# The seven-product stage of a decoder block: neighbouring pairs interleaved, weights requested further ahead, two tiles for the last sums

## The chip, the cores and the metric

The kernel runs on one core of a Trainium2 chip, as one launch. The time is device microseconds for the whole program. Engines are called as in the profile: PE (TensorE matmuls), DVE (VectorE), ACT (ScalarE), POOL (GpSimd) and SP (SyncE), which here only issues DMAs, from one queue and in order.

## The reference

One decoder block on x of 2048 tokens x 1024 channels, in float32. Two mixers (attention and a gated MLP) are merged and projected, then comes an MLP of width 4096, each with RMSNorm before and after. The stage of the change is the last part, above all the product with w_mlp_in:

```python
y = jnp.einsum('bsd,de->bse', merged, w_out[layer])
x = x + _rmsnorm(y, norm_post_mix[layer])

h = _rmsnorm(x, norm_pre_mlp[layer])
a = jax.nn.relu(jnp.einsum('bsd,df->bsf', h, w_mlp_in[layer]))
y = jnp.einsum('bsf,fd->bsd', a * a, w_mlp_out[layer])
x = x + _rmsnorm(y, norm_post_mlp[layer])
```

## The kernel before

**Precision.** Each float32 operand is split in two parts: a rounded copy (ACT, L71) and the rest (DVE, L76). Every product is three matmuls of such parts, so 128 x 512 outputs over four blocks of 128 channels take twelve.

**The last chunk.** Tokens come in four chunks of 512, in the order 2, 3, 0, 1; a chunk has four blocks of 128 (`out_block`, L764). A block loads x (tile xr), projects with w_out, normalizes, stores x1d (L791), then transposes y (L810) and ACT copies it (L811). In chunks 3 and 1 (`second`) it also loads the same columns of the chunk before from h2_d (L802), POOL makes sums of both (L815 to L818), and five 4-block groups (T1 to T4, B22) are stored to t_d (L820). For chunk 1 all four blocks use the first 20 slices of one tile, `tail`, so a block's loads wait for the store of the block before.

**The first MLP layer.** It is a Strassen-like scheme: the 1024 channels and each pair q of 128-wide weight columns (16 pairs) are halved, and seven products (`TERMS`, L840) take the place of eight. Each token half (half 1, then half 0) needs 16 x 7 = 112 products, 224 in all. For pair q, product 1 (A11 x B11) and 2 (A12 x B21) use bank a; 6, 7 and 4 (S2 x T2, S3 x T3, A22 x T4) bank b; 5 and 3 (S1 x T1, S4 x B22) bank c. A11 and A12 come straight from the raw weights w1r (`first_a`); S1 to S4 and A22 from four POOL sums (`sum_a`, L884 to L887). After 1 ACT copies the bank (xs, L915); after 6 and 7 DVE adds xs (u, L922); outputs are an add on DVE (c, L926), Relu on ACT (L927, or L918 after product 2), a square on POOL (L907) and a store sd (L908). These tiles are called c and form a ring of six.

**What sets the order.** PE runs in the order in which the program calls `product`. For each half this is a lead of five pairs (`ahead`: products 1 and 2 of all five, then `chain`: 6 to 3), a middle, pair by pair 1, 6, 2, 7, 5, 4, 3, and a trail of three pairs like the lead. Weights are made ready six products ahead (`need`), and raw weights are loaded there, into two w1r buffers; pairs of lead and trail load their first half alone (512 KB) and later all of it. The other engines' order, SP's queue too, is laid out by a scheduler from the dependences. Below, "6(0)" is product 6 of pair 0; in tile names the last digits are half and pair (S2_10 is half 1, pair 0; S2_115 half 1, pair 15).

## Time and profile before

| | |
|---|---|
| median of 3 runs | 2910.29 us (2909.26 to 2912.29) |
| the profiled execution | 2906.08 us |
| its span | 2904.3 us (1.78 us lie around it) |
| PE busy | 2802.4 us (96%) |
| DVE, ACT, POOL busy | 1463.8, 858.2, 765.1 us (50%, 30%, 26%) |
| mean granted clock of PE | 0.983 |
| first MLP layer: last matmul of the projection ends, first of the second layer begins | about 1498.6, 2195.14 us |

Times in rows are microseconds from the span's start. A wait is put down to what released it last. "x12" counts instructions that follow each other, and the duration is theirs together. L is a line of the kernel before.

### The profile page before, as it was taken

Reading aid. Unit: us, or ns where it says so; the run is one execution under the profiler, and the core shown is the slowest. Engines: PE = TensorE matmul, PEld = TensorE weight load, DVE = VectorE, ACT = ScalarE, POOL = GpSimd, SP = SyncE. Lnnn points to the kernel's source line nnn. Section 1 sums busy time; section 2 is a strip of 40 time slices with the busy share of each in tenths; the row PEclk is TensorE's granted clock in tenths of the full one; section 3 lists DMA queues with packets and bytes.
Section 4 is the critical chain, followed back from the end, with each engine's and each line's share of the span. In section 5 each row is a group of like instructions: output and inputs, shape, how many; then the busy total and the mean of one; then the engine's idle time right before and its main releaser. Section 6 shows DMA issues by size and latency. Waiting matters only on the chain.

```text
span 2904.3 us, 36721 instructions
## 1 busy us (share of the span) xinstructions
PE 2802.4 (96%) x13748; PEld 2359.1 (81%) x13748; DVE 1463.8 (50%) x2557; ACT 858.2 (30%) x1799; POOL 765.1 (26%) x591
## 2 busy tenths in 40 slices
PE   8999999999999999998987999899999999999998
PEld 8889889888888879787866787777878888888887
DVE  5664562444443354655556553565547444664445
ACT  4213111244443322443434333433332111211111
POOL 0340340200000032113125654265442010320012
PEclk9999999999999999999998999999999999999999
DMA  7544455566666363647456333633345232452232
GB/s 254 176 145 159 152 152 158 156 214 191 198 201 193 134 225 113 217 149 205 135 182 213 113 113 131 196 109 109 116 142 181 80 116 88 138 174 94 88 94 95
DMA packets 246546, 442.89 MB, mean 152 GB/s; under 512 B 17888, under 2 KB 106208, under 8 KB 246368
## 3 DMA queue, kind: packets, MB, share of 16 engines
q1 hardware_dynamic: 246368, 440.55, 47.2%
q8 instruction: 108, 1.77, 0.3%
q14 instruction: 70, 0.57, 0.1%
HBM read 299.77 MB, written 140.71 MB: 152 GB/s over the span
## 4 chain that ended last, share of the span: by engine, by line
PE 77%; DMA 7%; issue 4%; POOL 4%; DVE 4%; ACT 2%; SPq 0%; POOLq 0%; DVEq 0%; ACTq 0%
PE y L87 8%; PE y L86 8%; PE y L88 8%; PE ab L903 6%; PE ac L903 4%; PE aa L903 4%; PE g L86 4%; PE g L88 4%; PE g L87 4%; PE x L87 3%; PE x L86 3%; PE x L88 3%; DMA w1r<-in_w_mlp_in_dram 2%; PE pv L597 2%; DMA g<-gated 1%
## 5 line engine op out<-in xcount | busy, mean ns | idle before, releaser
L87 PE MATMUL y<-w,s 128*128 128x512 f32 x1024 | 400.1, 391 | 0.0
L86 PE MATMUL y<-w,s 128*128 128x512 f32 x1024 | 399.6, 390 | 0.0
L88 PE MATMUL y<-w,s 128*128 128x512 f32 x1024 | 398.8, 389 | 0.0
L71 ACT ACTIVATE s<-s 128x512 fp32r<-128x512 f32 x128 | 80.6, 632 | 495.3 <-DMA s<-sd 467.6
L86 PEld LDWEIGHTS y<-w,s 128*128 128x128 f32 x1024 | 192.3, 188 | 41.1
L88 PEld LDWEIGHTS y<-w,s 128*128 128x128 f32 x1024 | 192.3, 188 | 40.6
L87 PEld LDWEIGHTS y<-w,s 128*128 128x128 f32 x1024 | 192.5, 188 | 39.7
L1109 DVE TENSOR_TENSOR acc<-acc,y 128x512 f32<-128x512 f32 x240 | 159.5, 683 | 129.4 <-PE y L88 129.4
L903 PE MATMUL aa<-B,A 128*128 128x512 f32 x768 | 194.8, 410 | 24.1 <-ACT A L71 12.6
L907 POOL TENSOR_TENSOR c<-c 128x512 f32<-128x512 f32 x126 | 150.7, 1197 | 238.5 <-ACT c L927 176.0
L73 POOL TENSOR_SCALAR w<-w2r 128x1024 fp32r<-128x1024 f32 x64 | 69.6, 1088 | 528.3 <-DVE acc L1109 250.4
L903 PE MATMUL ab<-T,S 128*128 128x512 f32 x768 | 188.6, 398 | 14.6 <-DVE u L922 12.0
L903 PEld LDWEIGHTS aa<-B,A 128*128 128x128 f32 x768 | 151.9, 199 | 60.5 <-ACT A L71 13.6
L903 PEld LDWEIGHTS ab<-T,S 128*128 128x128 f32 x768 | 147.3, 192 | 48.1 <-DVE u L922 13.3
L86 PE MATMUL x<-hT_a,wq 128*128 128x512 f32 x384 | 149.8, 390 | 0.0
L88 PE MATMUL x<-hT_a,wq 128*128 128x512 f32 x384 | 149.6, 390 | 0.0
L87 PE MATMUL x<-hT_a,wq 128*128 128x512 f32 x384 | 149.6, 390 | 0.0
L76 DVE TENSOR_TENSOR A<-w1r,A 128x512 fp32r<-128x512 f32 x92 | 91.7, 1006 | 107.0 <-ACT A L71 106.4
L73 POOL TENSOR_SCALAR w_g<-w_g_r 128x1024 fp32r<-128x1024 f32 x32 | 33.6, 1049 | 411.0 <-PE g L88 329.4
L76 DVE TENSOR_TENSOR w<-w2r,w 128x1024 fp32r<-128x1024 f32 x64 | 82.2, 1285 | 115.6 <-POOL w L73 115.6
L604 DVE TENSOR_REDUCE o<-po 128x256 f32<-128x512 f32 x48 | 33.2, 691 | 184.1 <-PE po L603 184.1
L76 DVE TENSOR_TENSOR s<-s 128x512 fp32r<-128x512 f32 x128 | 90.0, 710 | 70.2 <-ACT s L71 69.9
(276 smaller groups left out, 6531.2 us busy)
## 6 DMA issues: line engine op xcount, KB each, us to landing
w1r<-in_w_mlp_in_dram SPq DMA_DIRECT2D x32, 1024.0 KB, 5.3
w2r<-in_w_mlp_out_dram SPq DMA_DIRECT2D x64, 512.0 KB, 3.6
s<-sd SPq DMA_DIRECT2D x128, 256.0 KB, 4.6
sd<-c SPq DMA_DIRECT2D x126, 256.0 KB, 2.7
qk<-hl SPq DMA_DIRECT2D x24, 1024.0 KB, 5.3
qq<-qk SPq DMA_DIRECT2D x96, 256.0 KB, 5.0
w_g_r<-in_w_in_dram SPq DMA_DIRECT2D x32, 512.0 KB, 5.3
gated<-gt SPq DMA_DIRECT2D x64, 256.0 KB, 3.1
```

The source lines that it names most:

```text
L71: act.activation(hi, src, AF.Copy)
L73: pool.tensor_scalar(hi, src, 1.0, 1.0, op0=OP.mult, op1=OP.mult)
L76: (pool if lo_eng == "pool" else dve).tensor_sub(lo, src, f32(hi))
L86: pe.matmul(ps, lh, rh, start=start, stop=False)
L87: pe.matmul(ps, lh, rl, start=False, stop=False)
L88: pe.matmul(ps, ll, rh, start=False, stop=stop)
L597: pe.matmul(pv[:, o0:o0 + w_], l, r, start=n == 0, stop=n == len(mms) - 1, skip_group_check=True)
L604: dve.tensor_reduce(ot[:, :, j * 64:(j + 1) * 64], po.rearrange("p (b h e) -> p b e h", b=4, h=2), axis=AX.X, op=OP.add)
L903: pe.matmul(p, w[:, l, k, :], h[:, r, k, :], start=i in (1, 6, 5) and not k and not n, stop=k == 3 and n == 2, skip_group_check=True)
L907: pool.tensor_mul(t, t, t)
L1109: dve.tensor_add(an, an, p)
```

## The change

It edits the last chunk's blocks, the loading of weights and the order of the products; no product is added or left out.

- The h2_d loads of a block are issued with its xr load; the t_d store becomes a third part of the block, run by `store()`. Chunk 1 alternates between two 20-slice parts of `tail`, which has 48 slices instead of 44.
- For pairs of lead and trail A11 and A12 are loaded apart, 256 KB each (`lone_a`), into c tiles; the first five of half 1 go through the last eight slices of `tail`, A11 of pair 2 among them.
- w1r has three buffers instead of two, and its loads are asked for 14 products ahead (`raw_need`); splits and sums still six ahead. A pair of lead or trail loads w1r once, whole.
- `places` gives every product a place in a list; both halves' lists are put into one by sorting. The T tiles are loaded in the order T2, T3, T1, T4, B22 (before T2, T1, T3, T4, B22).

```diff
--- before.py
+++ after.py
@@ -767,6 +767,12 @@
         isl = slice(i * P, (i + 1) * P)
         xt = tp.tile([P, D], F32, name=f"xr_{c}{i}", tag="xr", bufs=1)
         sp.dma_start(xt, x[t0:t0 + P, :])
+        second = c % 2
+        if second:
+
+            tt = tt_tile(c, i)
+            for o in range(2):
+                sp.dma_start(tt[:, 3 * o], h2_d[:, o * 4:o * 4 + 4, t0 - 512:t0 - 512 + P])
...
@@ -794,12 +800,6 @@
...
-        second = c % 2
-        if second:
-
-            tt = tt_tile(c, i)
-            for o in range(2):
-                sp.dma_start(tt[:, 3 * o], h2_d[:, o * 4:o * 4 + 4, t0 - 512:t0 - 512 + P])
...
@@ -816,16 +816,23 @@
...
+        yield
+        if second:
             dst = t_d[c // 2].rearrange("p o k t -> p (o k) t")[:, :, i * P:(i + 1) * P]
             sp.dma_start(dst, tt.rearrange("p o k t -> p (o k) t"))
         yield
 
-    last = [None]
+    last, stores = [None], []
 
     def flush():
         if last[0]:
             next(last[0])
+            stores.append(last[0])
             last[0] = None
+
+    def store():
+        while stores:
+            next(stores.pop(0))
 
     chunks = (2, 3, 0, 1)
     e3, er = ExitStack(), ExitStack()
@@ -859,23 +866,31 @@
...
+    def lone_a(half, q, n, raw=None):
+
+        w = r3.tile([P, 2, 4, P], F32R, name=f"A1{n + 1}_{half}{q}", tag="wh", bufs=5)
+        if raw is None:
+            raw = cp3.tile([P, 512], F32, name=f"ar{n}_{half}{q}", tag="c", bufs=6)
+            raw = raw.rearrange("p (k c) -> p k c", k=4)
+        split_in(w, a["w_mlp_in"][2 * q][:, n * 4:n * 4 + 4], raw, "act")
+        a_[half, q, f"A1{n + 1}"] = w
+
+    def first_a(half, q):
 
         for n, name in enumerate(("A11", "A12")):
             w = r3.tile([P, 2, 4, P], F32R, name=f"{name}_{half}{q}", tag="wh", bufs=5)
-            split(w[:, 0], w[:, 1], raw[:, n * 4:n * 4 + 4], "act", "dve")
+            split(w[:, 0], w[:, 1], araw[half, q][:, 0, n * 4:n * 4 + 4], "act", "dve")
             a_[half, q, name] = w
 
-    def load_a(half, q, n=2):
-
-        raw = wp3.tile([P, 2, KT, P], F32, name=f"w1r_{half}{q}", tag="w1r", bufs=2)
-        sp.dma_start(raw[:, :n].rearrange("p f k c -> p f (k c)"),
-                     a["w_mlp_in"][2 * q:2 * q + n].rearrange("f p k c -> p f (k c)"))
+    def load_a(half, q):
+        raw = wp3.tile([P, 2, KT, P], F32, name=f"w1r_{half}{q}", tag="w1r", bufs=3)
+        sp.dma_start(raw.rearrange("p f k c -> p f (k c)"),
+                     a["w_mlp_in"][2 * q:2 * q + 2].rearrange("f p k c -> p f (k c)"))
         araw[half, q] = raw
 
     def sum_a(half, q):
 
-        raw = araw.pop((half, q))
+        raw = araw[half, q]
...
@@ -934,19 +949,33 @@
...
-    def chain(qs, between):
-
-        o = [(qs[0], 6)]
-        for n, q in enumerate(qs):
-            o += [(q, 5), (q, 7)] + ([(qs[n + 1], 6)] if n + 1 < len(qs) else between) + [(q, 4), (q, 3)]
-        return o
-
-    def ahead(qs):
-
-        o = [(q, 1) for q in qs]
-        for n, q in enumerate(qs):
-            o.insert(min(2 * n + 2, len(o)), (q, 2))
-        return o
+    def places(half):
+
+
+
+        o = []
+
+        def ahead(qs, t0):
+            o.extend((t0 + t, q, 1) for t, q in zip((0, 1, 3, 5, 7), qs))
+            t = dict(zip(qs, (2, 4, 6, 8, 9)))
+            o.extend((t0 + t[q], q, 2) for q in qs)
+
+        def chain(qs, t0):
+            for n, q in enumerate(qs):
+                o.extend((t0 + 5 * n + t, q, i) for i, t in ((6, 0), (7, 3), (5, 4), (4, 6), (3, 7)))
+
+        ahead(range(LEAD), 0)
+        t0 = 2 * LEAD - 2.5
+        chain(range(LEAD), t0)
+        t0 += 5 * LEAD
+        for q in range(LEAD, NQ - TRAIL):
+            o.extend((t0 + t, q, i) for i, t in ((1, -0.25), (6, 1.25), (2, 3), (7, 5), (5, 6), (4, 9), (3, 11)))
+            t0 += 7
+        trail = range(NQ - TRAIL, NQ)
+        ahead(trail, t0 + 0.25)
+        t0 += 2 * TRAIL
+        chain(trail, t0)
+        return o, t0 + 5 * TRAIL
 
...
@@ -967,7 +996,7 @@
 
     def tt_tile(c, i):
         if c == 1:
-            return tail[:, :20].rearrange("p (o k) t -> p o k t", o=5)
+            return tail[:, i % 2 * 20:i % 2 * 20 + 20].rearrange("p (o k) t -> p o k t", o=5)
...
@@ -975,75 +1004,76 @@
     mg = merge(2, yt, {}, spatial_out)
     for n, c in enumerate(chunks):
         if n:
-            mg = merge(c, yt, {2: flush})
+            mg = merge(c, yt, {2: flush, 5: store})
         if n < 3:
             yt = load_y(chunks[n + 1])
         for i in range(4):
+            store()
+            if n == 3 and i == 0:
+                tail = yp.tile([P, 48, P], F32, name="tail", tag="yt")
             b = out_block(c, i, mg)
             next(b)
             flush()
             last[0] = b
-            if n == 3 and i == 0:
-                tail = yp.tile([P, 44, P], F32, name="tail", tag="yt")
             if n == 3 and i == 1:
                 e2r.close()
...
-                rw = tail[:, 20:].rearrange("p (n k) c -> p n k c", n=3)
-                for q in range(2):
-                    sp.dma_start(rw[:, q], a["w_mlp_in"][2 * q])
-                    first_a(1, q, rw[:, q])
-                    rls.append(rw[:, 2, q * 4:(q + 1) * 4].rearrange("p k t -> p (k t)"))
+                rls += [gtp.tile([P, 512], F32, name=f"c11_{o}", tag=f"gt{o}", bufs=2) for o in range(2)]
+                for o, (q, n_) in enumerate(((0, 0), (1, 0), (0, 1), (1, 1), (2, 0))):
+                    lone_a(1, q, n_, tail[:, 40 + o % 2 * 4:44 + o % 2 * 4])
 
 
     first_half, second_half = 1, 0
     for q, i in ((0, 1), (1, 1), (0, 2), (1, 2)):
         product(first_half, q, i)
     flush()
+    store()
     e2.close()
     ea = ExitStack()
...
-    order = []
-    for half in (first_half, second_half):
-        lead, trail = list(range(LEAD)), list(range(NQ - TRAIL, NQ))
-        o = ahead(lead) + chain(lead, [(LEAD, 1)])
-        for q in range(LEAD, NQ - TRAIL):
-            o += [(q, i) for i in (1, 6, 2, 7, 5, 4, 3) if (q, i) != (LEAD, 1)]
-        o += ahead(trail) + chain(trail, [])
-        order += [(half, q, i) for q, i in o if half != first_half or q > 1 or i > 2]
+    o, t_end = places(first_half)
+    order = [(t, first_half, q, i) for t, q, i in o if q > 1 or i > 2]
+    order += [(t + t_end, second_half, q, i) for t, q, i in places(second_half)[0]]
+    order = [z[1:] for z in sorted(order)]
 
     ends = {}
     for z in order:
         if z[0] == first_half:
             ends[TERMS[z[2]][1]] = z
-    have = {(first_half, q): {1} for q in range(2)}
+    have = {(first_half, 0, 1), (first_half, 1, 1), (first_half, 0, 2), (first_half, 1, 2), (first_half, 2, 1)}
+
+    def alone(q):
+        return q < LEAD or q >= NQ - TRAIL
 
     def need(half, q, i):
 
-        h = have.setdefault((half, q), set())
-        part = 1 if i < 3 else 2
-        if part in h:
+        if (half, q, i) in have:
             return
-        h.add(part)
-        alone = q < LEAD or q >= NQ - TRAIL
-        if part == 1:
-            load_a(half, q, 1 if alone else 2)
-            first_a(half, q, araw[half, q][:, 0])
-            if alone:
-                araw.pop((half, q))
+        if i < 3 and alone(q):
+            lone_a(half, q, i - 1)
+            have.add((half, q, i))
+        elif i < 3:
+            first_a(half, q)
+            have.update(((half, q, 1), (half, q, 2)))
         else:
-            if (half, q) not in araw:
-                load_a(half, q)
             sum_a(half, q)
-
-    tops = ["T2", "T1", "T3", "T4", "B22"]
+            have.update((half, q, n) for n in range(3, 8))
+
+    def raw_need(half, q, i):
+        if (half, q) not in araw and not (i < 3 and alone(q)):
+            load_a(half, q)
+
+    tops = ["T2", "T3", "T1", "T4", "B22"]
     for n, z in enumerate(order):
         if tops:
             load_t(first_half, tops.pop(0))
+        for z2 in order[n:n + 14]:
+            raw_need(*z2)
         for z2 in order[n:n + 6]:
             need(*z2)
         product(*z)
```

On PE, at the start of the first half, the kernel before ran all products 1 and 2 of the lead and then pair 0's 6 (ab_10 with T2), 5 (ac_10 with T1) and 7 (T3):

```order
L903 MATMUL aa_13_13330<-B11_1_12923,A11_13_13272 128x512 x12
L903 MATMUL aa_12_13286<-B21_1_12930,A12_12_13267 128x512 x12
L903 MATMUL aa_14_13375<-B11_1_12923,A11_14_13280 128x512 x12
L903 MATMUL aa_13_13330<-B21_1_12930,A12_13_13275 128x512 x12
L903 MATMUL aa_14_13375<-B21_1_12930,A12_14_13283 128x512 x12
L903 MATMUL ab_10_13451<-T2_1_13255,S2_10_13310 128x512 x12
L903 MATMUL ac_10_13466<-T1_1_13301,S1_10_13312 128x512 x12
L903 MATMUL ab_10_13451<-T3_1_13345,S3_10_13311 128x512 x12
L903 MATMUL ab_11_13520<-T2_1_13255,S2_11_13399 128x512 x12
L903 MATMUL ab_10_13451<-T4_1_13368,A22_10_13313 128x512 x12
```

And now, from the same product 1(3) on:

```order
L918 MATMUL aa_13_13343<-B11_1_12924,A11_13_13274 128x512 x12
L918 MATMUL aa_12_13314<-B21_1_12931,A12_12_13279 128x512 x12
L918 MATMUL aa_14_13388<-B11_1_12924,A11_14_13284 128x512 x12
L918 MATMUL ab_10_13430<-T2_1_13263,S2_10_13289 128x512 x12
L918 MATMUL aa_13_13343<-B21_1_12931,A12_13_13309 128x512 x12
L918 MATMUL aa_14_13388<-B21_1_12931,A12_14_13338 128x512 x12
L918 MATMUL ab_10_13430<-T3_1_13329,S3_10_13290 128x512 x12
L918 MATMUL ac_10_13493<-T1_1_13358,S1_10_13291 128x512 x12
L918 MATMUL ab_11_13531<-T2_1_13263,S2_11_13410 128x512 x12
L918 MATMUL ab_10_13430<-T4_1_13381,A22_10_13292 128x512 x12
```

Product 6(0) has moved ahead of 2(3) and 2(4), 7(0) ahead of 5(0), with two products between 6(0) and 7(0) where there was one, two between 7(0) and 4(0) where there was one, and two between 5(0) and 3(0) where there were three.

On PE, at the passage from half 1 to half 0, before (pair 15 of half 1 ends, then products 1 and 2 of half 0):

```order
L903 MATMUL ab_115_15367<-T3_1_13345,S3_115_15267 128x512 x12
L903 MATMUL ab_115_15367<-T4_1_13368,A22_115_15269 128x512 x12
L903 MATMUL ac_115_15439<-B22_1_13390,S4_115_15270 128x512 x12
L903 MATMUL aa_00_15549<-B11_0_15149,A11_00_15408 128x512 x12
L903 MATMUL aa_01_15564<-B11_0_15149,A11_01_15433 128x512 x12
L903 MATMUL aa_00_15549<-B21_0_15210,A12_00_15411 128x512 x12
L903 MATMUL aa_02_15603<-B11_0_15149,A11_02_15487 128x512 x12
L903 MATMUL aa_01_15564<-B21_0_15210,A12_01_15436 128x512 x12
L903 MATMUL aa_03_15656<-B11_0_15149,A11_03_15543 128x512 x12
```

And now:

```order
L918 MATMUL ab_115_15387<-T3_1_13329,S3_115_15282 128x512 x12
L918 MATMUL ac_115_15476<-T1_1_13358,S1_115_15283 128x512 x12
L918 MATMUL aa_00_15506<-B11_0_15151,A11_00_15382 128x512 x12
L918 MATMUL aa_01_15526<-B11_0_15151,A11_01_15409 128x512 x12
L918 MATMUL ab_115_15387<-T4_1_13381,A22_115_15284 128x512 x12
L918 MATMUL aa_00_15506<-B21_0_15242,A12_00_15450 128x512 x12
L918 MATMUL ac_115_15476<-B22_1_13403,S4_115_15285 128x512 x12
L918 MATMUL aa_02_15642<-B11_0_15151,A11_02_15501 128x512 x12
L918 MATMUL aa_01_15526<-B21_0_15242,A12_01_15521 128x512 x12
L918 MATMUL aa_03_15685<-B11_0_15151,A11_03_15543 128x512 x12
L918 MATMUL aa_02_15642<-B21_0_15242,A12_02_15572 128x512 x12
```

The first products of half 0 stand between the last of half 1, and 6(0) of half 0 (ab_00) comes before the last two of its products 2.

On SP, the end of the last chunk, before (xr_13 is the last block's x, td its sums, tail its h2 columns, w1r raw weights, B and T the stage's inputs):

```order
L769 DMA xr_13_13055<-in_x_dram 128x1024
L820 DMA td_81<-tail_12810 2560x1x128
L791 DMA x1d_79<-xr_13_13055 128x1024
L802 DMA tail_12810<-h2d_80 128x4x128 x2
L908 DMA sd_82<-tail_12810 128x512
L872 DMA w1r_12_13262<-in_w_mlp_in_dram 128x1024
L908 DMA sd_82<-tail_12810 128x512
L820 DMA td_81<-tail_12810 2560x1x128
L872 DMA w1r_13_13270<-in_w_mlp_in_dram 128x1024
L872 DMA w1r_14_13278<-in_w_mlp_in_dram 128x1024
```

And now:

```order
L775 DMA tail_12725<-h2d_80 128x4x128 x2
L769 DMA xr_13_13065<-in_x_dram 128x1024
L822 DMA td_81<-tail_12725 2560x1x128
L797 DMA x1d_79<-xr_13_13065 128x1024
L923 DMA sd_82<-c11_1_12939 128x512
L82 DMA ar0_13_13275<-in_w_mlp_in_dram 128x512
L82 DMA ar1_12_13280<-in_w_mlp_in_dram 128x512
L82 DMA ar0_14_13285<-in_w_mlp_in_dram 128x512
L923 DMA sd_82<-c11_0_12938 128x512
L887 DMA w1r_10_13270<-in_w_mlp_in_dram 128x2x1024
L822 DMA td_81<-tail_12725 2560x1x128
L887 DMA w1r_11_13272<-in_w_mlp_in_dram 128x2x1024
```

The last block's tail loads and xr no longer stand on either side of the td store of the block before but both ahead of it; three lone pieces (ar0, ar1) and the whole w1r of pair 0 stand ahead of the last td store.

## Rows read from the trace of the kernel before

**Rows 1.** Waits of PE, 1500 to 2200: waited for, us, times, longest

```profile
PE ab L903 <- DVE u L922: 22.4, 11, 6.3
PE aa L903 <- ACT A L71: 12.6, 2, 9.2
PE aa L903 <- ACT xs L915: 11.4, 3, 4.8
```

**Rows 2.** Windows: bounds, us, PE busy (x), granted clock, DMA share, GB/s

```profile
1498.60:1582.00 83.40, 57.38 (x210) 0.84 0.67 221
1582.00:1660.20 78.20, 71.87 (x314) 1.00 0.38 125
1660.20:1790.00 129.80, 129.80 (x571) 1.00 0.32 112
1790.00:1903.00 113.00, 98.31 (x392) 0.91 0.53 174
1903.00:2130.00 227.00, 221.18 (x960) 0.99 0.34 113
2130.00:2195.10 65.10, 62.15 (x264) 0.97 0.42 141
```

**Rows 3.** Timeline of PE, stage's start: start, us, what, [idle before <-releaser]

```profile
1500.46 1.77 PE L810 MATMUL pt<-ident,y 128*128 128x128 f32 x8 [1.85 <-DVE y L795]
...
1513.94 4.62 PE L903 MATMUL aa<-B,A 128*128 128x512 f32 x12 [2.60 <-ACT xs L915]
...
1528.62 5.49 PE L903 MATMUL aa<-B,A 128*128 128x512 f32 x12 [9.19 <-ACT A L71]
...
1566.51 6.16 PE L903 MATMUL ab<-T,S 128*128 128x512 f32 x14 [6.34 <-DVE u L922]
```

**Rows 4.** Timeline of PE, end of half 1 and first of half 0

```profile
1793.95 4.59 PE L903 MATMUL ac<-B,S 128*128 128x512 f32 x12 [2.45 <-DVE c L926]
...
1870.89 21.80 PE L903 MATMUL aa<-B,A 128*128 128x512 f32 x84 [4.05 <-ACT xs L915]
1897.47 5.49 PE L903 MATMUL aa<-B,A 128*128 128x512 f32 x12 [4.78 <-ACT xs L915]
```

**Rows 5.** Chain of waits, last chunk: start, us, what

```profile
1498.62 6.21 DMA td<-tail
...
1508.13 1.29 POOL tail L815
...
1514.28 6.21 DMA td<-tail
...
1528.94 7.91 DMA w1r<-in_w_mlp_in_dram
```

**Rows 6.** Timeline of ACT, block 1 of the last chunk

```profile
1488.31 1.09 ACT L811 ACTIVATE tail<-pt 128x512 f32<-128x512 f32 x2 [0.94 <-DMA td<-tail]
```

**Rows 7.** Timeline of SP's queue, last chunk and first T loads

```profile
1506.17 0.34 SPq L769 DMA_DIRECT2D xr<-in_x_dram  x1
...
1535.18 1.77 SPq L82 DMA_DIRECT2D T<-td  x4
```

**Rows 8.** DMA issues, 1500 to 2190: count, KB each, median us to landing

```profile
w1r<-in_w_mlp_in_dram SPq DMA_DIRECT2D x32, 1024.0 KB, 5.3
sd<-c SPq DMA_DIRECT2D x123, 256.0 KB, 2.7
...
w1r<-in_w_mlp_in_dram SPq DMA_DIRECT2D x14, 512.0 KB, 4.1
```

**Rows 9.** Timeline of DVE, splits of half a T or B22 tile

```profile
1540.63 1.23 DVE L76 TENSOR_TENSOR T<-T 128x1024 fp32r<-128x1024 f32 x1 [0.52 <-ACT T L71]
...
1563.58 2.28 DVE L76 TENSOR_TENSOR B<-B 128x1024 fp32r<-128x1024 f32 x1
```

**Rows 10.** Waits of SP, 1590 to 1790

```profile
SPq L908 <- POOL c L907: 143.9, 42, 9.2
```

**Rows 11.** Groups of POOL, 1500 to 2190: busy us, mean ns

```profile
L907 POOL TENSOR_TENSOR c<-c 128x512 f32<-128x512 f32 x123 | 147.1, 1197 | 230.6 <-ACT c L927 168.1 <-ACT c L918 62.1
L887 POOL TENSOR_TENSOR w1r<-w1r 128x512 f32<-128x512 f32 x32 | 50.1, 1566 | 2.2
```

More of the change, by code (lines that the diff above doesn't have):

```diff
@@ L860, in load_t @@
         b_[half, name] = w
-    def first_a(half, q, raw):
+    def lone_a(half, q, n, raw=None):
[6 more added lines that the diff above has]
+    def first_a(half, q):
         for n, name in enumerate(("A11", "A12")):
             w = r3.tile([P, 2, 4, P], F32R, name=f"{name}_{half}{q}", tag="wh", bufs=5)
-            split(w[:, 0], w[:, 1], raw[:, n * 4:n * 4 + 4], "act", "dve")
+            split(w[:, 0], w[:, 1], araw[half, q][:, 0, n * 4:n * 4 + 4], "act", "dve")
             a_[half, q, name] = w
-    def load_a(half, q, n=2):
-        raw = wp3.tile([P, 2, KT, P], F32, name=f"w1r_{half}{q}", tag="w1r", bufs=2)
-        sp.dma_start(raw[:, :n].rearrange("p f k c -> p f (k c)"),
-                     a["w_mlp_in"][2 * q:2 * q + n].rearrange("f p k c -> p f (k c)"))
+    def load_a(half, q):
+        raw = wp3.tile([P, 2, KT, P], F32, name=f"w1r_{half}{q}", tag="w1r", bufs=3)
+        sp.dma_start(raw.rearrange("p f k c -> p f (k c)"),
+                     a["w_mlp_in"][2 * q:2 * q + 2].rearrange("f p k c -> p f (k c)"))
         araw[half, q] = raw
     def sum_a(half, q):
-        raw = araw.pop((half, q))
+        raw = araw[half, q]
         a11, a12, a21, a22 = (raw[:, f, k:k + 4] for f in range(2) for k in (0, 4))
```

## The prediction

> **What bounds the kernel now.** I read the page's engine table first: TensorE (PE) is busy 96% of the span, so only its gaps and its slow stretches can be won. Then the waits of PE inside the seven-product stage [rows 1]: 11 waits of 22.4 us for the sums u on VectorE, 12.6 us for weight splits A on ScalarE, 11.4 us for the copies xs. Then the stage cut into windows [rows 2]. The reader should see there one window without loss: 1660 to 1790, 129.80 us busy out of 129.80 at clock 1.00, 571 matmuls. 571 / 12 = 47.6 products, so a product of twelve matmuls costs 2.73 us. The stage has 224 products and 16 short transposes (1.77 us for the eight that stand alone in [rows 3], estimate 2 us together): 224 x 2.73 + 2 = 613.5 us. It takes 1498.6 to 2195.1 = 696.5 us. So 83 us are lost, as waits and as matmuls at a lower granted clock behind waits, and this is all the change can reach.
>
> Where they are lost, window by window (length minus products x 2.73; products counted as matmuls / 12, partly counted ones left to their window): 1498.6 to 1582.0 holds 16 products and the transposes, 45.7 us of work in 83.4: **37.7 lost**. 1582.0 to 1660.2 holds 26 products, 71.0 in 78.2: **7.2**. 1790 to 1903 holds 32.6 products, 89 in 113: **24**, of which 2.45 of wait and some 1.7 of slow matmuls (4.59 us for twelve) are the single wait for c at 1793.95 [rows 4], so 4.1 and 19.9. 1903 to 2130: 227.0 with 960 matmuls (80 products, 218.4) leaves 8.6, of which the page of waits names u; I count **7.2**. After 2130: **6**. These five add to 82.
>
> **The first 16 products.** The last chunk's four blocks share one 20-slice tile. In the chain of waits [rows 5] the reader should see it go round: td store of 6.21 us from 1498.62, then loads of h2 into the same tile, four sums on GpSimd from 1508.13 to 1514.28, a store of 6.21 again, and at the end a w1r load of 7.91 that began only at 1528.94. PE meanwhile stood 9.19 us before product 1(2) and 6.34 before 7(0) [rows 3]. (I write product i of pair q as i(q).) With two tiles and the loads issued at the block's start, the sums of block 1 no longer wait for store and loads of block 0. ScalarE copies their transposes at 1488.31 and waited 0.94 us for that store [rows 6], so they begin near 1488 and take about 6.1 us (1508.13 to 1514.28): store at 1494.1 instead of 1498.62, 4.5 us earlier. The same queue carries x1d and then the next xr, which is issued at 1506.17 [rows 7]: xr now goes at about 1501.6, and y of the last block is ready 4.5 us earlier too, near 1512. ScalarE's copy xs of 1(1) stood behind that chain; its 2.60 us [rows 3] go, and products 1(0), 1(1), 2(0), 2(1) end at about 1514.1 rather than 1518.4. The transposes follow to 1515.2.
>
> A11 of pair 2 is now among five pieces loaded into the tail tile before the stage, so 1(2) starts at 1515.2 rather than 1528.62. The pieces for 1(3), 2(2), 1(4) stand behind one sd store whose square is done near 1513.5; with 2.7 us for 256 KB [rows 8] and two splits of some 0.6 each (half of the 1.23 of a tile twice as wide, [rows 9]) they are there at 1518, when 1(2) ends. So 1(4) ends at 1515.2 + 4 x 2.73 = 1526.1. What is late next is T2. The last td store leaves when the sums of block 3 end, 1515.2 + 6.1 = about 1521.3 instead of 1528.37; T2 lands 6.2 + the queue later, 1528, where before its loads were only issued at 1535.18 [rows 7]; its splits (1.23 to 2.28 a half on VectorE [rows 9], as much again with ScalarE's part ahead) end near 1533.5. In the new order 6(0) stands before 2(3) and 2(4), so PE waits 1533.5 - 1526.1 = 7.4 us with two ready products queued behind it. Then 6(0), 2(3), 2(4) to 1545.4 (a little lost to a lower clock and to VectorE, which splits T3, T1 meanwhile), four products to 1556, then 3(0) with its B22 on a backlogged VectorE to about 1561.5. **16 products at 1561.5 instead of 1582.0: 20.5 us.** Bounds: 8, if the T splits all run at the slower rate and every wait in the list returns in half; 28, if 6(0) waits 3 us and nothing else does. I take the middle, since each step has a row.
>
> **The lead chains.** In the five lead pairs a pair takes five products, 13.6 us. Their 7.2 us come from a circle: a w1r load of 5.3 us [rows 8] issued behind an sd store that waits for GpSimd's square (143.9 us of such waits of SP between 1590 and 1790 [rows 10]), four GpSimd sums, five splits, then u. Third w1r buffer and a look 14 products ahead put the load some two pairs earlier, so its 5.3 us leave the circle. What is left is GpSimd itself: four sums of about 1.5 and four squares of 1.2 [rows 11] are 10.8 of 13.6 us, which fits with little to spare. The new order leaves two products instead of one between 6 and 7 and between 7 and 4, and two instead of three between 5 and 3. I let 2.0 us of 7.2 remain: **5.2**, and **5.2** in the second half's lead chain (bounds 0 and 7.2 each). The single wait for c at the end of each middle stretch: product 3 needs the bank that 5 left, two products later, and the sum c stood on VectorE behind splits for the next pair; now four products lie between 5 and 3. 4.1 go in the first half, and 4.5 of 6 in the second (1.5 left for u). Bounds 0 and 10 for both.
>
> **The transition.** Two waits of 4.05 and 4.78 us for xs and the slow matmuls behind them [rows 4] come from the place between the halves: ten products 1 and 2 in a row on ScalarE, T and B loads and a w1r load that waited for squares. In the changed order the first half's last six products alternate with the second half's products 1 and 2, and A pieces stand at least two products ahead in SP's queue, T loads about 13. I leave 4 of 19.9: **15.8** (bounds 8 and 19.9).
>
> **Added work.** Sixteen DMA issues more, 0.34 us each on SP as for xr [rows 7], which mostly waits; no more matmuls, and the same splits. A lone 256 KB load costs its landing, 2.7 against 4.1 for 512 KB [rows 8]; two of them end together about where one did, beside PE's 2.73 us per product. Zero, covered by the two products ahead; without cover each would be a wait of 2.7. The Trainium skill, "DMA: Bandwidth & Descriptors", Anatomy of one DMA, speaks against this edit: a fixed part of about 2 us per DMA and the bytes on top. The rows agree in kind (2.7, 4.1, 5.3 for 256, 512 and 1024 KB). By it the two pieces would hold the queue longer in sum; it would matter only were they not issued ahead.
>
> **Sum.** 20.5 + 5.2 + 4.1 + 15.8 + 5.2 + 4.5 = 55.3 us. The profiled run took 2906.08 (span 2904.3 and 1.78 around it), so 2850.8; it stood 4.2 under the median 2910.29, and the median moves alike: **2855**. About 27 of the 83 lost us remain, mostly before 1562. The forecast's own range: all upper bounds give 28 + 7.2 + 10 + 19.9 + 7.2 = 72, time 2838; three quarters of the sum give 2869. I take 2842 to 2866 for it.
>
> **Rivals.**
> A. VectorE takes over at the start. The split of half a tile took 1.23 us at 1540.63 and 2.28 at 1563.58, beside GpSimd's sums [rows 9]. Now the T splits fall just where GpSimd makes the sums of pairs 0 and 1. Ten T and B22 splits at 2.28 instead of 1.23 are 10.5 us more, on the path of 6(0), 5(0), 3(0): the start gains 20.5 - 11 = 9, time 2866. Against: GpSimd worked there before too. The Trainium skill, "SBUF — State Buffer", SBUF: two separate sides, says why such pairs could exclude each other: the shared port pair is locked for a whole instruction. The long splits agree with that.
> B. GpSimd holds the lead chains and the transition. If squares and sums, 10.8 of 13.6 us, come at the wrong time, u stays late: the lead chains give nothing, the transition half: 55.3 - 10.4 - 8 = 37, time 2873. For: SP's longest waits are for GpSimd [rows 10]; against: a fifth of it is free.
> C. Slower. The lone pieces share the ring of six c tiles with the outputs. Each waits until a tile's square is made and its store has landed, in SP's one ordered queue: ScalarE then waits for the piece, and xs and PE behind. Both halves have 27 such loads. A landing of 2.7 us [rows 8] waited for at each is 73 us lost against 55 won: time 2910 + 18 = 2928; it decides from 2 us at each, and the two xs waits [rows 4] are that kind of wait at twice the size. Against: the loads stand two or more products ahead (5.5 us).
> D. The change doesn't do what it says at the start: 6(0) ahead of 2(3) and 2(4) gives the gain back (T2 later than 1541 and the first 16 products as before): 55.3 - 20.5 = 34.8, time 2875.
>
> **Chances.** Forecast 0.52, A 0.17, B 0.13, D 0.06, C 0.07, and 0.05 that several of A, B and D together leave nothing to see. 0.2% (6 us) is about what a measurement of this kernel can tell from no change. Faster 0.52 + 0.17 + 0.13 + 0.06 = 0.88, same 0.05, slower 0.07. Range 2842 to 2889: it takes in A, B and D, and leaves out C, the "nothing", and gains over 68.
>
> **What would show it.** Right: last td store at about 1521, 1(2) straight behind the transposes, one wait of some 7 us before 6(0), 16 products done near 1562, no xs wait between the halves, waits for u under 5 us in all (from 22.4), the second layer's first matmul near 2140. Wrong: a wait for T or B splits of more than 10 us (A); waits for u unchanged with w1r loads early (B); ScalarE waiting for ar loads at many places (C); 16 products after 1575 (D).

## The result: 1.8% faster, a little less than forecast

| | before | changed |
|---|---|---|
| median | 2909.78 us (4 runs) | 2858.38 us (2853.53 to 2859.65, 4 runs) |
| ratio of the times, 95% interval | | 0.9822 (0.9805 to 0.9839) |
| span of the profiled execution | 2904.3 us | 2856.3 us |
| first MLP layer, from the projection's last matmul to the second layer's first | 1498.6 to 2195.1 = 696.5 us | 1499.9 to 2147.4 = 647.5 us |

The forecast was 2855 in a range of 2842 to 2889. Everything behind the stage is unchanged: from the second layer's first matmul to the end of the span it was 709.2 us before and is 708.9 now. The part ahead of the stage ended 1.3 us later in this execution, so the spans differ by 48.0 where the stage differs by 49.0.

First the waits of PE in the stage of the changed kernel (waited for, us, times, longest), which answer to [rows 1]:

```profile
PE ab L918 <- ACT T L71: 6.3, 2, 5.6
PE aa L918 <- ACT A L71: 5.5, 3, 3.4
PE ab L918 <- DVE u L937: 3.6, 2, 1.9
PE ab L918 <- DVE T L76: 1.7, 2, 0.9
PE aa L918 <- ACT xs L930: 1.5, 2, 1.1
PE aa L918 <- DVE A L76: 1.3, 2, 0.9
```

In [rows 1] u, A and xs made 46.4 us; here they are 10.6, and the largest entry is new: 5.6 us once for ScalarE's split of a T tile. The windows of the same trace, with cuts moved to where products end (columns as in [rows 2]):

```profile
1498.60:1567.10 68.50, 55.42 (x214) 0.88 0.80 271
1567.10:1660.20 93.10, 93.10 (x411) 1.00 0.37 125
...
1790.00:1875.00 85.00, 78.57 (x331) 0.96 0.57 192
1875.00:2100.00 225.00, 225.00 (x990) 1.00 0.35 118
```

Two of these windows are full: 93.10 of 93.10 and 225.00 of 225.00, clock 1.00. They hold both lead chains and the second middle stretch, which lost time in [rows 2]. Nearly all that is left stands before 1567 and between 1790 and 1875. A granted clock of 1.00 is TensorE's upper level (2.4 GHz), 0.50 its lower one (1.2 GHz); a window shows the mean.

The start on PE (L918 is the products' matmul):

```profile
1514.51 3.01 PE L918 MATMUL aa<-B,A 128*128 128x512 f32 x12
1518.47 0.73 PE L918 MATMUL aa<-B,A 128*128 128x512 f32 x2 [0.96 <-ACT A L71]
1520.06 8.02 PE L918 MATMUL aa<-B,A 128*128 128x512 f32 x34 [0.85 <-DVE A L76]
1533.65 0.80 PE L918 MATMUL ab<-T,S 128*128 128x512 f32 x1 [5.56 <-ACT T L71]
1535.37 2.50 PE L918 MATMUL ab<-T,S 128*128 128x512 f32 x5 [0.93 <-DVE T L76]
1538.63 0.79 PE L918 MATMUL ab<-T,S 128*128 128x512 f32 x1 [0.76 <-ACT T L71]
1540.15 2.50 PE L918 MATMUL ab<-T,S 128*128 128x512 f32 x5 [0.73 <-DVE T L76]
```

Product 1(2) follows the transposes at 1514.51. It stood at 1528.62 in [rows 3]. Then 1(3), 2(2) and 1(4) run, and at 1533.65 product 6(0) begins after 5.56 us of wait. It stops three times more, 0.93, 0.76 and 0.73: for the rest of the tile's first half, and for both splits of its second half. Its twelve matmuls take until 1542.5. The 16th product ends at 1567.1, before at 1582.0.

### The profile page after: what moved, and what is told of

The parts are those of the page before. It is cut to its first block, busy times and chain, and to the rows that moved or that the text cites. A ratio compares the mean times of both kernels' runs of the same rounds, so it can differ in the third digit from the quotient of the medians.

```text
span 2856.3 us, 36699 instructions
## 1 busy us (share of the span) xinstructions
PE 2787.4 (98%) x13748; PEld 2347.7 (82%) x13748; DVE 1464.7 (51%) x2557; ACT 861.0 (30%) x1799; POOL 760.5 (27%) x591
## 4 chain that ended last, share of the span: by engine, by line
PE 80%; DMA 6%; DVE 4%; POOL 4%; issue 4%; ACT 2%; SPq 0%; DVEq 0%; POOLq 0%; ACTq 0%
PE y L87 8%; PE y L86 8%; PE y L88 8%; PE ab L918 7%; PE ac L918 5%; PE aa L918 4%; PE g L88 4%; PE g L86 4%; PE g L87 4%; PE x L86 3%; PE x L87 3%; PE x L88 3%; PE pv L597 2%; DMA g<-gated 1%; PE pT L578 1%
## 5 line engine op out<-in xcount | busy, mean ns | idle before, releaser
L918 PE MATMUL aa<-B,A 128*128 128x512 f32 x768 | 191.6, 402 | 8.4 <-ACT A L71 5.5
L918 PE MATMUL ab<-T,S 128*128 128x512 f32 x768 | 188.7, 394 | 9.8 <-ACT T L71 6.3
L918 PEld LDWEIGHTS aa<-B,A 128*128 128x128 f32 x768 | 147.6, 193 | 44.9 <-ACT A L71 6.8
L918 PEld LDWEIGHTS ab<-T,S 128*128 128x128 f32 x768 | 145.4, 190 | 42.9 <-ACT T L71 7.5
L71 ACT ACTIVATE S<-w1r 128x512 fp32r<-128x512 f32 x96 | 60.2, 631 | 154.9 <-PE ab L918 88.5
```

What stands on the lines that cost most here:

```text
L71: act.activation(hi, src, AF.Copy)
L918: pe.matmul(p, w[:, l, k, :], h[:, r, k, :], start=i in (1, 6, 5) and not k and not n, stop=k == 3 and n == 2, skip_group_check=True)
```

## Where the runs differ: the loss, cut by products

The profiled executions reached the stage's start at different times (1495.7 to 1504.5 us), while what follows the stage took 708.9 to 709.7 us in all of them. So I compare the stage itself. In each trace I count products along PE's timeline, and take from each stretch 2.73 us per product (and 2 us for the transposes). The numbers are us lost; a stretch is uncertain by about 1, since a group of matmuls that a window cuts is counted at both ends; the last column is too high by some 1.5 in every row. A loss is waits of PE and matmuls at the lower granted clock together. "Again" is the changed kernel a second time.

| kernel | stage | 1-16 | 17-42, lead | 43-134, passage | 135-212, lead | 213-224 |
|---|---|---|---|---|---|---|
| before | 696.5 | 37.7 | 6.6 | 24.1 | 11.1 | 3.6 |
| changed | 647.5 | 21.5 | -0.5 | 9.5 | -0.1 | 3.7 |
| again | 647.6 | 21.3 | -0.6 | 8.4 | -0.1 | 5.1 |
| e2 two buffers, 6 ahead | 673.2 | 20.0 | 11.8 | 18.3 | 6.5 | 3.1 |
| e3 halves not mixed | 646.6 | 18.9 | -0.6 | 10.7 | -0.1 | 4.2 |
| e4 6(0) later | 643.5 | 20.9 | -0.3 | 6.4 | -0.1 | 3.1 |
| e5 old order | 650.5 | 20.8 | -0.6 | 11.3 | 1.8 | 3.7 |
| e6 three buffers, 6 ahead | 639.5 | 16.1 | -0.3 | 6.4 | -0.1 | 4.0 |
| e7 one tile, late loads | 651.5 | 28.8 | -0.5 | 6.3 | -0.1 | 3.5 |
| e8 whole first halves | 644.3 | 26.0 | -0.6 | 2.1 | -0.1 | 3.4 |
| e9 before, three buffers | 673.5 | 37.5 | -0.6 | 18.4 | 1.3 | 3.5 |

In the passage the changed kernel, "again", e4, e6 and e7 run the same instructions in the same order on every engine, and lose 6.3 to 9.5 us. So differences of up to 3 us there are not put down to an edit.

## The experiments

Ratios are to the kernel before on the same chip, with 95% intervals; the changed kernel itself measured 0.9817 (0.9802 to 0.9832) in the last group (run "again").

**e1. One tile, loads at the block's start.**

```diff
-            return tail[:, i % 2 * 20:i % 2 * 20 + 20].rearrange("p (o k) t -> p o k t", o=5)
+            return tail[:, :20].rearrange("p (o k) t -> p o k t", o=5)
```

> The changed kernel with one 20-slice tile for the last sums again (loads of h2 still issued at the block's start). Theory (each part of the change pays in its own place; the two tiles pay at the start): the td store of a block must land before the next block's h2 loads, the last td store leaves at about 1528 instead of 1521.19, product 6(0) starts 6 to 8 us later than 1533.65, and from 1600 on the trace is unchanged: 2858 + 7 to 10 = 2866 to 2868. Rival (the start is set by the weights: the 9.43 us w1r load behind the td store and GpSimd's sums for S2): 6(0) starts within 2 us of 1533.65, time 2857 to 2861.

Ratio 0.9855 (0.9838 to 0.9872). In this kernel the next block's h2 loads overwrite the columns of the block before ahead of its sums, since those loads now stand before these sums in the program. It computes something else, so it isn't the case that was meant. Run e7 puts the question again.

**e2. Two w1r buffers, requested 6 ahead.**

```diff
-        raw = wp3.tile([P, 2, KT, P], F32, name=f"w1r_{half}{q}", tag="w1r", bufs=3)
+        raw = wp3.tile([P, 2, KT, P], F32, name=f"w1r_{half}{q}", tag="w1r", bufs=2)
...
-        for z2 in order[n:n + 14]:
+        for z2 in order[n:n + 6]:
```

> The changed kernel with two w1r buffers and raw weights asked for 6 products ahead again. Theory (early loads pay in the lead chains): waits for u come back between 1567 and 1660 and between 1875 and 2000, 5 to 7 us in each: 2868 to 2873. Rival (two products between 6 and 7 and between 7 and 4 are enough by themselves): both windows stay without loss, within 3 us of 2858.

Ratio 0.9918 (0.9904 to 0.9933), 2882.39 us: slower than the theory said, 2868 to 2873. The chain of waits in its first lead (start, us, what) shows the circle:

```profile
1588.46 0.74 DVE S L76
1589.20 6.37 DMA w1r<-in_w_mlp_in_dram
...
1604.59 0.81 DVE S L76
1605.41 6.03 DMA w1r<-in_w_mlp_in_dram
...
1619.37 1.50 POOL c L922
1620.88 0.32 SPq L923
1621.30 6.17 DMA w1r<-in_w_mlp_in_dram
```

Two of these three w1r loads start when VectorE has made the last split of an earlier pair, which frees the buffer (1588.46 and 0.74, then 1589.20). Such a load lands 6.37 later, splits and u follow, and the next one starts at 1605.41, 16.2 us after the last; five products are 13.6 us. The third, at 1621.30, leaves behind an sd store that waited for its square on GpSimd. PE waits for u (us, times, longest in the stage):

```profile
PE ab L918 <- DVE u L937: 16.5, 7, 3.3
```

**e3. Halves one behind the other.**

```diff
-    order = [z[1:] for z in sorted(order)]
+    order = [z[1:] for h in (first_half, second_half) for z in sorted(z for z in order if z[1] == h)]
```

> The changed kernel with the two halves' product lists one behind the other instead of mixed. Theory (mixing pays at the passage between the halves): ten products 1 and 2 in a row again, waits for xs and A between 1830 and 1900 grow by 7 to 12 us: 2865 to 2870. Rival (T loads behind sd stores set the passage, and the mixing is beside the point): the window 1790 to 1880 loses 8 to 12 us as in the changed kernel, time 2856 to 2861.

Ratio 0.9834 (0.9821 to 0.9847); the passage loses 10.7 against 6.3 to 9.5 with the halves mixed. The theory's 7 to 12 us don't come: mixing is worth 1 to 4 us at most, and the time doesn't show them. The rival has the time and the loss right; that T loads behind sd stores set the passage is not shown by this run. The largest wait of its passage, 3.6 us, is put down to ScalarE's split of a T tile.

**e4. 6(0) behind 2(3) and 2(4).**

```diff
-        t0 = 2 * LEAD - 2.5
+        t0 = 2 * LEAD - (2.5 if half != first_half else 0)
```

> The changed kernel with product 6(0) of the first half moved behind 2(3) and 2(4), and 7(0) straight behind 6(0). Theory (6(0) waits 8.0 us for T2 while two ready products stand behind it): 5 us of that wait are covered, 1 to 2 us come back as a wait of 7(0) for u: 2854 to 2856. Rival (T2, S2 and the last A12 pieces come over the same queue and the same splits, so the wait only moves to 2(4) or 7(0)): 2857 to 2861.

Ratio 0.9818 (0.9803 to 0.9832), as the changed kernel; products 1 to 16 lost 20.9 against 21.5. The rival holds, and PE's timeline shows what I had not seen: 2(3) was not ready either.

```profile
1535.73 1.22 PE L918 MATMUL aa<-B,A 128*128 128x512 f32 x2 [10.58 <-ACT A L71]
```

PE waits 10.58 us for A12 of pair 3. ScalarE's timeline in the same trace, around that split:

```profile
1533.59 0.63 ACT L71 ACTIVATE S<-w1r 128x512 fp32r<-128x512 f32 x1 [2.51 <-POOL w1r L901]
1534.12 1.04 ACT L71 ACTIVATE T<-T 128x1024 fp32r<-128x1024 f32 x1
1535.07 1.13 ACT L71 ACTIVATE A<-ar 128x512 fp32r<-128x512 f32 x2
```

The A splits (1535.07) stand in ScalarE's order behind a split of S for pair 1, which waits 2.51 us for GpSimd's sums until 1533.59. The piece itself was issued at 1526.33 and took 5.2 us to land, so it lay ready from about 1531.6: some 3.5 of the 10.58 us are ScalarE's order, the rest is the late piece.

**e5. The old order with the new loads.** `places` gives way to the old `chain` and `ahead`, with the T tiles in the old order; the rest of the change stays.

> The changed kernel with the order of products (and of the T tiles) of the kernel before, all its new loads and tiles kept. Theory (early raw weights feed the lead chains; with two w1r buffers each w1r load waited for the splits of an earlier pair, 16 us a pair): no loss in 1567 to 1660 and 1875 to 2000 even in the old order, only the single waits for c (4 us each) come back: 2858 to 2866. Rival (the two products between 6 and 7 and between 7 and 4 are as necessary as the loads): 5 to 7 us of waits for u in each lead chain and the waits for c: 2870 to 2880.

Ratio 0.9837 (0.9815 to 0.9859), stage 3.0 us longer. Products 17 to 42 lose nothing. The theory holds, and of the two forecast waits for c one of 0.2 us comes back (another, of 0.5, falls in the first lead). Its largest waits are 11.0 us for A12 before 2(3), as in e4, and 5.9 us for u at the passage.

**e6. Three buffers, 6 ahead.**

```diff
-        for z2 in order[n:n + 14]:
+        for z2 in order[n:n + 6]:
```

> The changed kernel with three w1r buffers, but raw weights asked for only 6 products ahead. Theory (the third buffer is what frees the load, the rest is order in the program): 2857 to 2863. Rival (the early request is what matters; six products ahead a load of 5.3 us and four sums of 5.8 just don't fit beside the splits): waits for u in the lead chains as in the run with two buffers, 2872 to 2885.

Ratio 0.9805 (0.9785 to 0.9825), 2850.67 us. Neither theory nor rival expected it faster than the changed kernel. Against e2, one buffer apart, the stage is 33.7 us shorter: the third buffer does it, and the early request nothing. By time e6 and the changed kernel can't be told apart (the intervals overlap); by the traces the stage is 8 us shorter, 5 of them in the first 16 products and the rest in the passage, within its spread. The first 16 products as one window (columns as in [rows 2]), the changed kernel, then e6:

```profile
1499.90:1567.10 67.20, 54.12 (x209) 0.87 0.80 271
1496.40:1558.20 61.80, 50.27 (x209) 0.92 0.83 285
```

PE's waits are 67.20 - 54.12 = 13.1 us and 61.80 - 50.27 = 11.5 us. So waits make 1.6 of the 5.4 us, and the larger part is matmuls at the lower granted clock. Its SP queue there:

```profile
1517.26 4.85 SPq L82 DMA_DIRECT2D ar<-in_w_mlp_in_dram  x2
1522.15 0.48 SPq L887 DMA_DIRECT2D w1r<-in_w_mlp_in_dram  x1
1524.31 2.75 SPq L82 DMA_DIRECT2D T<-td  x6
```

and the same place in the changed kernel:

```profile
1521.19 0.52 SPq L822 DMA_DIRECT2D td<-tail  x1
1521.76 3.26 SPq L887 DMA_DIRECT2D w1r<-in_w_mlp_in_dram  x1
1528.79 0.81 SPq L82 DMA_DIRECT2D T<-td  x2
1529.66 0.42 SPq L82 DMA_DIRECT2D ar<-in_w_mlp_in_dram  x1
1530.18 0.86 SPq L82 DMA_DIRECT2D T<-td  x2
1531.09 0.43 SPq L887 DMA_DIRECT2D w1r<-in_w_mlp_in_dram  x1
1531.56 0.47 SPq L82 DMA_DIRECT2D ar<-in_w_mlp_in_dram  x1
```

The w1r load of pair 1 stands before T2 in both (1521.76 and 1522.15). With 14 ahead the pieces of A12 stand behind T2, at 1529.66 and 1531.56, the second one also behind the w1r load of pair 2 (1531.09). With 6 the two pieces go from 1517.26 on, and the T pieces close together from 1524.31.

**e7. One tile, loads and store as before.** The tail tile, the place of the h2 loads and the store in the second part are those of the kernel before.

> The changed kernel with the last chunk's blocks as before: one 20-slice tile, h2 loads after the projection, td store in the same part. Theory (two tiles pay at the start): last td store near 1528 instead of 1521.19, product 6(0) 6 to 8 us later, nothing else: 2864 to 2868. Rival (S2 of pair 0 and the w1r loads set the start): 6(0) within 2 us, 2855 to 2860.

Ratio 0.9858 (0.9836 to 0.9880), 2865.49 us, in the theory's range. Counted from the stage's start the last td store leaves after 29.5 us (1531.40) against 21.3, and PE starts 6(0) after 43.2 (1545.11) against 33.7, 9.5 us later where the theory had 6 to 8. Products 1 to 16 lose 28.8 against 21.5, so the theory has the place right. The stage is only 4.0 us longer, since the passage lost 6.3 here, so that the time fits is in part luck. The run takes back three things at once, the second tile, the early loads and the later store; which of them gives the 7 us is not shown.

**e8. A11 and A12 together.** One 512 KB buffer for them, and a ring of 4 c tiles instead of 6.

```diff
+    def pair_a(half, q):
+        raw = wp3.tile([P, KT, P], F32, name=f"hr_{half}{q}", tag="hr", bufs=1)
+        sp.dma_start(raw, a["w_mlp_in"][2 * q])
...
-        if i < 3 and alone(q):
+        if i < 3 and alone(q) and (half, q) != (first_half, 2):
+            pair_a(half, q)
```

> The changed kernel with A11 and A12 of the lead and trail pairs loaded together again, 512 KB in one extra buffer, for all pairs but the first half's 0 to 2; the ring of c tiles has 4 instead of 6, so the room is the same. Theory (two lone pieces or one load cost the same where they are asked for six products ahead): 2855 to 2862. Rival (the pieces pay, since the first is there 1.4 us before a whole load and no slot waits for the other's split): a wait for A of 3 us or more at each of the three leads and trails behind the start, 2864 to 2875. Other rival (pieces in the outputs' ring wait for stores): 2848 to 2854.

Ratio 0.9837 (0.9819 to 0.9856). In sum the same, by two opposite parts: at the start 26.0 lost against 21.5 (one wait of 20.1 us for A before 1(3), in place of several), at the passage 2.1 against 6.3 to 9.5. So the pieces pay at the start, and at the passage this kernel is 4 to 7 us better. At the start the whole load of pair 3 leaves SP's queue at 1532.69, behind T2, where the pieces leave from 1513.76 on; so the place in the queue differs there and not the size alone. The room for outputs changed too, so what makes the difference at the passage is not settled.

**e9. The kernel before with a third buffer.**

```diff
-        raw = wp3.tile([P, 2, KT, P], F32, name=f"w1r_{half}{q}", tag="w1r", bufs=2)
+        raw = wp3.tile([P, 2, KT, P], F32, name=f"w1r_{half}{q}", tag="w1r", bufs=3)
```

> The kernel before with one edit: three w1r buffers instead of two. Theory (the third buffer is the largest part of the gain; taking it away cost 26 us of the stage): the lead chains' 7 us each and part of the passage between the halves go, 14 to 25 us: 2881 to 2893. Rival (in the kernel before the half-filled w1r loads of lead and trail take buffers too, so the third one pays only with the lone pieces): 0 to 6 us, 2900 to 2907.

Ratio 0.9907 (0.9890 to 0.9923), 2881.32 us, as the theory has it: one number gives half of what the change gives. The stage is 23.0 us shorter. PE's waits in it:

```profile
PE ab L903 <- DVE u L922: 16.1, 8, 6.3
PE aa L903 <- ACT A L71: 12.6, 2, 8.3
```

u falls from 22.4 to 16.1, A stays at 12.6 [rows 1], and the table has 37.5 us lost in the first 16 products as before: the start and part of the passage are not the buffer's.

**e10 and e11. 6 or 8 ahead with a later 6(0).** e10 has the edit of e6, and 6(0) between 2(3) and 2(4); e11 asks 8 ahead and has the edit of e4.

> The changed kernel with raw weights asked for 6 products ahead (three buffers kept) and product 6(0) of the first half between 2(3) and 2(4). Theory (with 14 ahead the w1r load of pair 1 stood on the queue before the last A12 pieces and T2; with 6 these pieces are early, so 2(3) covers part of the wait for T2): 2 to 3 us less than the run with 6 ahead alone, ratio to the kernel before about 0.9795, 2847. Rival (u of 6(0) comes one product later and 7(0) waits): the same as 6 ahead alone, ratio 0.9805.

> The changed kernel with raw weights asked for 8 products ahead and 6(0) behind both 2(3) and 2(4). Theory: the A12 pieces are early, both products run while T2 comes, 7(0) waits 1 to 2 us for u: ratio about 0.978 to 0.979, 2843 to 2846. Rival (as above, the wait only moves): ratio 0.9805 or more.

Ratios 0.9822 (0.9807 to 0.9836) and 0.9817 (0.9802 to 0.9831), stages 643.3 and 644.6: neither is better than e6. PE waits 4.4 us for A in e10 and 3.6 us for a T split before 7(0) in e11. The wait moves on. In the first 16 products PE's waits are nearly those of e6 (12.1 and 12.4 us against 11.5), but the mean granted clock is 0.90 and 0.87 against 0.92; why the clock is lower is not settled. By time the three can't be told apart.

**Again.**

> The changed kernel as it is, beside the others on one chip: ratio to the kernel before within 0.9805 to 0.9839, the interval of its first measurement. If it comes out under 0.9805, the gain of the run with 6 ahead is not told from it.

Ratio 0.9817 (0.9802 to 0.9832), within that interval.

## Why the prediction was nearly right

Its terms against the stage's 49.0 us, the measured ones from the table above:

| term | forecast | measured |
|---|---|---|
| first 16 products | 20.5 | 37.7 - 21.5 = 16.2 |
| first lead chain | 5.2 | 6.6 + 0.5 = 7.1 |
| first c wait and passage | 4.1 + 15.8 = 19.9 | 24.1 - 9.5 = 14.6 |
| second lead chain, second c wait, end | 5.2 + 4.5 = 9.7 | 11.1 + 0.1 + 3.6 - 3.7 = 11.1 |

The side was right, and so were two of the mechanisms: the early sums at the start (e7) and the third buffer in the lead chains (e9). Steps of three terms were not, and their errors partly cancel: start and passage came 9.6 us short, the other two rows 3.3 over. One figure of the count before was also off: behind 2130 its own rule gives 65.1 - 22 x 2.73 = 5.0 lost, not 6.

**The start.** The steps on the queue hold to a microsecond: td store of block 1 at 1494.43 (forecast 1494.1), xr at 1502.14 (1501.6), last td store at 1521.19 (1521.3). 6(0) began at 1533.65 (1533.5), but that is luck. The forecast has T2 landed at 1528 and both its halves split by 1533.5. T2's loads were only issued at 1528.79, and the first took 3.7 us; the sum has no term for that. PE began when the first half's split by ScalarE was done, and the second half was not split until after 1537.54.

What failed is "with two ready products queued behind it" and "6(0), 2(3), 2(4) to 1545.4". The A12 pieces of the two products were issued at 1529.66 and 1531.56, behind T2, and e4 shows that they were not ready. The three products had 11.9 us in the sum and took 19.9 (columns as in [rows 2]):

```profile
1533.60:1553.50 19.90, 15.81 (x37) 0.60 0.81 284
```

Waits are 19.90 - 15.81 = 4.1 us of it. Three products at full clock are 8.2, so some 7.6 us are the lower clock, which was granted after PE had stood 5.56 us before 6(0): the window's mean is 0.60. The sum had 3.7 for both, as "a little lost to a lower clock and to VectorE". Against these 8.0 us stand a wait for B22 of 2.5 that didn't come and a 6(0) that began 1.2 earlier, counted from the stage's start; 4.3 are missing in the end. Of the 16.2 that came, e7 shows 7.3 to be the blocks' new loads and stores; how the rest divides between the pieces loaded early and the order is not shown. ScalarE's timeline in the changed kernel:

```profile
1532.54 1.06 ACT L71 ACTIVATE T<-T 128x1024 fp32r<-128x1024 f32 x1 [1.58 <-issue]
1536.48 1.15 ACT L71 ACTIVATE S<-w1r 128x512 fp32r<-128x512 f32 x2 [2.88 <-POOL w1r L901]
1537.54 1.04 ACT L71 ACTIVATE T<-T 128x1024 fp32r<-128x1024 f32 x1
```

The second half's split (1537.54) stands behind two splits of S for pair 1, which wait 2.88 us for GpSimd. That is not the price of the look 14 products ahead: with 6 ahead (e6) ScalarE has the same order and nearly the same wait:

```profile
1533.32 1.15 ACT L71 ACTIVATE S<-w1r 128x512 fp32r<-128x512 f32 x2 [2.41 <-POOL w1r L901]
```

No run moved that split alone, so its price stays open. I had read SP's queue for what each load waits for, but not ScalarE's order for what each split stands behind.

**The lead chains.** They went whole, more than forecast, and for one reason where I gave three. The step "Third w1r buffer and a look 14 products ahead put the load some two pairs earlier" is right for the buffer (e9: 7.2 us of the first chain and 9.8 from 135 to 212 with nothing else changed; e2 against e6: loss in both comes back) and wrong for the look (e6). I named the square that SP's queue waits for. It does hold a load now and then (e2, 1621.30), but SP's waits for squares (same stretch and columns as [rows 10]) are as long as ever:

```profile
SPq L923 <- POOL c L922: 143.2, 42, 7.8
```

143.2 us against 143.9, with no loss on PE. A long wait of an ordered queue says little while the loads behind it are early. Nor are two products between 6 and 7 needed for it (e5).

**The passage.** I left 4 us and 9.5 stayed (8.4 in the second execution). What failed is the step "A pieces stand at least two products ahead in SP's queue, T loads about 13". SP's longest wait for a square (1828 to 1842: us, times, longest) and its queue, then ScalarE, then PE in the changed kernel:

```profile
SPq L923 <- POOL c L922: 9.7, 2, 5.0
```

```profile
1836.87 0.32 SPq L923 DMA_DIRECT2D sd<-c  x1
1837.24 0.42 SPq L82 DMA_DIRECT2D T<-td  x1
1837.76 1.35 SPq L82 DMA_DIRECT2D ar<-in_w_mlp_in_dram  x3
```

```profile
1842.94 1.06 ACT L71 ACTIVATE T<-T 128x1024 fp32r<-128x1024 f32 x1 [5.14 <-DMA T<-td]
1843.90 0.61 ACT L71 ACTIVATE A<-ar 128x512 fp32r<-128x512 f32 x1
```

```profile
1844.57 16.74 PE L918 MATMUL aa<-B,A 128*128 128x512 f32 x60 [3.35 <-ACT A L71]
```

The three A pieces leave from 1837.76 on, behind an sd store that waited 5.0 us for its square. PE had done what stands ahead of the next product at about 1841.2, 3.5 us later, and a piece took longer to land:

```profile
DMA to landing us min/median/max: 5.8/6.0/6.2
```

So the first piece was there at about 1843.6, its split went at 1843.90, and PE waited 3.35 us. ScalarE's T split ahead of it, 5.14 us late itself, held the A split for 0.3 us at most. The pieces stood two products ahead in the order of the queue but 3.5 us in time, and the landing was 5.8 where the sum took 2.7. Waits for u and xs (1.86 and 1.09 us) make the passage's waits 6.3 in all; the rest is matmuls at a lower granted clock, 0.96 in the mean from 1790 to 1875.

The 14.6 us that went didn't go for the reasons that I gave either. The third buffer is the largest part: without it the passage loses 18.3 (e2) where it loses 6.4 with it (e6), and in the kernel before it alone brings 24.1 down to 18.4 (e9). Mixing the halves gives 1 to 4 (e3), the whole new order 2 to 5 (e5). The wait for c, which I had put down to the two products between 5 and 3, is gone in the old order too: PE waits for no c in e9, and 0.2 us at the second place in e5.

**The rivals.** A: two T splits took 4.52 us together at 1549.37 of the changed kernel, while GpSimd made sums, where one took 1.21 at 1540.63, but PE waited 1.7 us for VectorE's T splits in all. So the long splits that the Trainium skill's "SBUF — State Buffer" (SBUF: two separate sides) would lead one to expect were there, and mostly off the path. B: GpSimd's 10.8 of 13.6 us do fit; neither chain loses time. C: ScalarE waits eight times for pieces, 10.1 us in the stage, and the kernel with whole loads gains 4 to 7 us at the passage (e8): the mechanism exists, at a tenth of the 73 us. D: the start kept 16.2. A piece's landing was 2.7 us in the forecast; 27 of them took 3.5 (median), five at the start 4.9. The Trainium skill's "DMA: Bandwidth & Descriptors" (Anatomy of one DMA — SWDGE (gpsimd) path) spoke against the pieces, though that section is on DMAs issued from GpSimd and these are issued from SP; in e8 the passage agrees, the start doesn't, and the sum decides nothing.

## What to carry to other kernels

Where a load starts right after the last reader of a buffer, try one more buffer before reordering: here that one number gave 23 of 49 us alone, and 34 in the new order. Asking for loads still earlier gained nothing here (e6), and it put a later load ahead of an urgent one on the queue. When a wait is to be covered by "ready" work, follow that work's inputs through every ordered queue and engine, ScalarE's too, and ask when they land and not only in which order they leave. Price a wait with the matmuls behind it: at the start the lower clock cost 7.6 us, more than the 5.56 us of wait before it.

## What the hardware showed beside this

A 1024 KB w1r load took 5.3 us in the median of the stage [rows 8], but 8.9 (median of five) from 1500 to 1567 of the changed kernel, where the DMA share was 0.80; it was 0.37 in the window after. One took 9.43. And the two executions of equal code differed mostly ahead of the stage: in the two profiles of the changed kernel it began at 1499.9 and 1498.6, with stages of 647.5 and 647.6 us.
